# A two-layer transformer step on one core: low weight parts from a copy of the high parts in PSUM, and a seventh bank

## The chip, the cores and the metric

The kernel runs on one core of one Trainium2 chip. The metric is the device time of one execution in microseconds (us). Three runs of the kernel before gave 3073.89, 3075.67 and 3076.87 us; the median is 3075.67. One execution was also recorded by the hardware profiler, which gives the span and the rows below.

## What is computed

The reference is one inference step of a network of two layers for 128 context tokens and 512 sample tokens (together 640 columns) with 1024 features. Each layer has a half-step SwiGLU, a token mixer, and another half-step SwiGLU, so there are four half-steps in all. The part that the change is about is this (the mixers, attention with a long convolution in the first layer and a gated DeltaNet in the second, stay as they are):

```
def half_ffn(x, g, mod, j, w13, w2):
    gt, up = split(ada_norm(x, g, mod, j) @ w13, 2)      # 1024 -> 2 x 2816
    return x + 0.5 * gate * ((silu(gt) * up) @ w2)       # 2816 -> 1024
```

`ada_norm` is an RMS norm followed by a scale and a shift that come from a conditioning vector, one for the context tokens and one for the sample tokens. All of it is in float32.

## The kernel before

**Number format.** TensorE multiplies in a rounded format (float32r). To keep float32 accuracy each operand is split into a high part, which is the value rounded, and a low part, which is the value less the high part. A product is then three matmuls: high times high, high times low, low times high. The weights are split on the chip, unit by unit.

**The weight stream.** `w_ahead` (L430 to L457) converts weight units in the order in which the products use them, up to five slots ahead of TensorE, in a ring of six slots of 1024 columns (`wh`). A unit of the up projection is 128 x 512 (four tiles of 128 x 128). For it ScalarE writes the high part (L452) and VectorE subtracts it from the source and so writes the low part (L453). Both of the subtraction's operands lie in SBUF. For each pair of tiles GpSimd first makes four sums and differences of the weights (L447), from which four of the seven units are taken. A number called priority moves these two instructions 30 places ahead in the scheduler's order; the copies of L783 are moved by 150. The order of the instructions on each engine is fixed when the program is built, and each engine works through its own in order.

**Up stages.** `ffn_s` (L741 to L830) is one half-step. The 22 pairs of a gate tile and an up tile (128 features each) are done in chunks of 7, 7 and 8, the up stages. A pair is not four products of halves in eight parts but seven, of Strassen's kind: q = 0 to 6, each 12 matmuls of 128 x 322 (four operand tiles, three matmuls each). The 322 columns are one half of the tokens, 320, and two columns that carry the shift of the modulation through the product, one for context and one for sample tokens, which serve as the biases. The products run in the order 0, 3, 4, 1, 5, 2, 6, and in the first pair of a half-step in the order 0, 3, 1, 2, 4, 5, 6.

The results lie in PSUM banks: a (q = 0 and 1), c (q = 3 and 2), d (q = 4, and q = 6 again), e (q = 5). These are banks 4, 5, 6, 7, but in the second pair of a half-step 2, 3, 0, 1:

```
a, c, d, e = [self.ps[:, b, :] for b in ((2, 3, 0, 1) if ci == 0 and m == 1 else range(4, 8))]
dst = (a, a, c, c, d, e, d)[q]
```

What reads them, in the order of a pair: ScalarE copies the partial results of q = 0 and q = 3 to SBUF (L783). VectorE adds d to the first copy (L789) and does the two bias columns by themselves (L791). After q = 1 it multiplies a by the norm's factor (L798) and copies the bias (L800). After q = 5 it adds e (L793, bias L794), and GpSimd adds the second copy and multiplies by the factor (L795, L796). After q = 2 VectorE adds c (L802) and multiplies by the factor (L803), both into SBUF, and ScalarE applies SiLU in two pieces, to the 128 context columns (L804) and the 512 sample columns (L805). After q = 6 VectorE adds d (L807, bias L808) and GpSimd multiplies by the factor (L809). `finish` (L755 to L759) then multiplies the two branches (L756, L757), ScalarE rounds the result (L758) and VectorE makes its low part (L759); it runs in the next pair, at q = 3.

**Factors of the norm.** In half-steps 2 to 4 the norm's factors are made late: `make_rstd` (L697 to L713) runs after q = 4 of the first pair, with two matmul groups in banks 0 and 1, a square root on ScalarE (L708), two reciprocals (L709) and two products (L711) on VectorE. In the first half-step the factors are 1, and 48 pieces of the modulation (`ada_small`, L569 to L592) are computed beside the products, with banks 0 and 1 as their ring: small matmuls (L582), a copy by ScalarE (L584), a transpose by TensorE (L587).

**The stages that follow.** After each chunk come eight output tiles of the down projection, each in two banks (0 and 1, or 2 and 3; `wide`, L400 to L403; `gemm`, L473 to L486), added to the residual by three VectorE instructions (`x_add`, L734 to L738, recorded as L737). The second half-step's three up stages are at 1056 to 1163, 1212 to 1304 and 1352 to 1458 us of the span.

## Time and profile before

| | |
|---|---|
| median of three runs | 3075.67 us (3073.89 to 3076.87) |
| span of the profiled execution, which is its own time | 3072.3 us, 3.4 below that median |
| mean granted TensorE clock | 0.978 of full speed |
| instructions | 54018 |
| DMA | 300.80 MB, 98 GB/s on average |

PE is TensorE with its matmuls, PEld its weight loads, DVE is VectorE, ACT ScalarE, POOL GpSimd and SP the engine that issues the transfers. A group of instructions is named by its line, engine, operation and tiles, and has its count, busy time and mean duration; behind the last bar stands the idle time of the engine just before these instructions and what ended it. The releasers are inferred from semaphore events. The end of a pipelined matmul is modelled, so a group of matmuls can be drawn a little longer than the time until the next one starts. TensorE's granted clock is given in parts of its full speed.

### The profile page before, as it was taken

Reading aid. Unit: us, or ns where it says so; the run is one execution under the profiler, and the core shown is the slowest. Engines: PE = TensorE matmul, PEld = TensorE weight load, DVE = VectorE, ACT = ScalarE, POOL = GpSimd, SP = SyncE. Lnnn points to the kernel's source line nnn. Section 1 sums busy time; section 2 is a strip of 40 time slices with the busy share of each in tenths; the row PEclk is TensorE's granted clock in tenths of the full one; section 3 lists DMA queues with packets and bytes.
Section 4 is the critical chain, followed back from the end, with each engine's and each line's share of the span. In section 5 each row is a group of like instructions: output and inputs, shape, how many; then the busy total and the mean of one; then the engine's idle time right before and its main releaser. Section 6 shows DMA issues by size and latency. Waiting matters only on the chain. (4 is left out here: it accounts for less than half of the span.)

```text
span 3072.3 us, 54018 instructions
## 1 busy us (share of the span) xinstructions
PE 2903.3 (94%) x20612; PEld 2683.4 (87%) x20612; DVE 2263.2 (74%) x5235; ACT 1303.0 (42%) x2678; POOL 1158.2 (38%) x955
## 2 busy tenths in 40 slices
PE   5999999999989899999999999999998999999999
PEld 3999999977766899999899999978878888899999
DVE  6858586687865785858785858679898967858584
ACT  4424243466522342424342424445555544424241
POOL 3525253101222563535563535332222224626361
PEclk7999999999989999999999999999999999999999
DMA  5434353334375122222122222322211112222222
GB/s 202 141 107 150 105 158 121 122 105 125 100 274 206 63 72 84 85 74 89 50 74 85 84 75 84 131 91 70 72 59 34 34 37 94 68 77 74 84 70 83
DMA packets 109439, 300.80 MB, mean 98 GB/s; under 512 B 11803, under 2 KB 31963, under 8 KB 104444
## 3 DMA queue, kind: packets, MB, share of 16 engines
q1 hardware_dynamic: 109180, 297.35, 29.1%
q8 instruction: 162, 2.65, 0.4%
q14 instruction: 97, 0.79, 0.1%
HBM read 277.38 MB, written 19.93 MB: 97 GB/s over the span
## 5 line engine op out<-in xcount | busy, mean ns | idle before, releaser
L453 DVE TENSOR_TENSOR wh<-base,wh 128x512 fp32r<-128x512 f32 (+2 forms) x746 | 745.7, 1002 | 122.0 <-PE psum L482 62.6
L452 ACT ACTIVATE wh<-base 128x512 fp32r<-128x512 f32 (+2 forms) x779 | 533.7, 706 | 669.1 <-PE psum L482 400.8
L447 POOL TENSOR_TENSOR base<-base 128x512 f32<-128x512 f32 x352 | 518.1, 1476 | 683.9 <-DMA base<-w 364.1
L482 PE MATMUL psum<-G,wh 128*128 128x320 f32 x4992 | 742.5, 310 | 8.5 <-DVE base L737 8.0
L482 PEld LDWEIGHTS psum<-G,wh 128*128 128x128 f32 x4992 | 737.0, 188 | 13.4 <-issue 7.5
L778 PE MATMUL psum<-H,wh 128*128 128x322 f32 x4224 | 700.7, 317 | 22.6 <-ACT H L659 11.8
L778 PEld LDWEIGHTS psum<-H,wh 128*128 128x128 f32 x4224 | 648.0, 192 | 41.6 <-ACT H L659 13.8
L778 PE MATMUL psum<-HX,wh 128*128 128x322 f32 x3168 | 527.5, 316 | 27.5 <-DVE base L808 21.7
L778 PEld LDWEIGHTS psum<-HX,wh 128*128 128x128 f32 x3168 | 482.0, 191 | 44.0 <-issue 31.8
L482 PE MATMUL psum<-H,wh 128*128 128x322 f32 (+1 forms) x2448 | 476.7, 330 | 3.6 <-DVE base L722 2.1
L482 PEld LDWEIGHTS psum<-H,wh 128*128 128x128 f32 x2448 | 375.3, 193 | 25.8 <-issue 17.7
L737 DVE SCALAR_TENSOR_TENSOR base<-psum,base 128x128 f32<-128x128 f32 x336 | 127.1, 433 | 211.6 <-PE psum L482 211.5
L453 POOL TENSOR_TENSOR wh<-base,wh 128x1024 fp32r<-128x1024 f32 x33 | 82.2, 2491 | 239.5 <-ACT wh L452 234.8
L795 POOL TENSOR_TENSOR base<-base 128x320 f32<-128x320 f32 x88 | 113.1, 1285 | 143.4 <-DVE base L794 133.6
L805 ACT ACTIVATE base<-base 128x512 f32<-128x512 f32 x88 | 63.6, 723 | 204.0 <-DVE base L803 204.0
L758 ACT ACTIVATE G<-base 128x640 fp32r<-128x640 f32 x88 | 65.1, 740 | 167.0 <-DVE base L757 156.8
L756 DVE SCALAR_TENSOR_TENSOR base<-base 128x128 f32<-128x128 f32 x88 | 32.9, 374 | 120.0 <-POOL base L809 120.0
L694 POOL TENSOR_TENSOR base<-base 128x640 f32<-128x640 f32 x30 | 77.7, 2589 | 110.9 <-ACT base L692 94.7
L796 POOL TENSOR_TENSOR base<-base 128x320 f32<-128x320 f32 x88 | 87.8, 998 | 6.9
L809 POOL TENSOR_TENSOR base<-base 128x320 f32<-128x320 f32 x88 | 76.2, 866 | 28.9 <-DVE base L808 28.9
L803 DVE TENSOR_TENSOR base<-base 128x320 f32<-128x320 f32 x88 | 85.1, 967 | 0.4
L759 DVE TENSOR_TENSOR G<-base,G 128x640 fp32r<-128x640 f32 x88 | 71.8, 816 | 15.0 <-ACT G L758 14.9
(702 smaller groups left out, 3764.6 us busy)
## 6 DMA issues: line engine op xcount, KB each, us to landing
base<-w SPq DMA_DIRECT2D x208, 512.0 KB, 3.2
base<-ada_w SPq DMA_DIRECT2D x128, 256.0 KB, 3.7
base<-w SPq DMA_DIRECT2D x64, 448.0 KB, 3.3
base<-dn_in SPq DMA_DIRECT2D x33, 512.0 KB, 3.3
base<-ada_w SPq DMA_DIRECT2D x14, 1024.0 KB, 5.0
G<-ada_w SPq DMA_DIRECT2D x48, 256.0 KB, 3.5
HX<-ada_w SPq DMA_DIRECT2D x10, 1024.0 KB, 4.9
base<-mx_in SPq DMA_DIRECT2D x18, 512.0 KB, 3.3
```

What stands on the lines that cost most here:

```text
L447: nc.gpsimd.tensor_tensor(out=out, in0=x, in1=y, op=op)
L452: nc.scalar.activation(out=hi, in_=src, func=AF.Copy)
L453: (self.lo_eng if q is None else nc.vector).tensor_tensor(out=lo, in0=src, in1=hif, op=ALU.subtract)
L482: nc.tensor.matmul(ps[:, h, :n], lhsT=w[:, k, :], rhs=m[k][:, HALF * h:HALF * h + n], start=start and k == 0 and w is hi and m is mh, stop ...
L694: nc.gpsimd.tensor_tensor(out=self.acc.f, in0=self.acc.f, in1=sq, op=ALU.add)
L737: nc.vector.scalar_tensor_tensor(out=xt[:, xo:xo + n], in0=ps[:, h, o:o + n], scalar=gate[:, t, c:c + 1], in1=xt[:, xo:xo + n], op0=ALU.mu ...
L759: TT(out=gl[m], in0=tu, in1=gf[m], op=ALU.subtract)
L778: nc.tensor.matmul(dst[:, :HB], lhsT=w[:, i, :], rhs=v[:, i, :], start=not more and i == 0 and n == 0, stop=i == 3 and n == 2, skip_group_ ...
L795: nc.gpsimd.tensor_tensor(out=p5, in0=u2[:, 0, :HALF], in1=p5, op=ALU.add)
L796: nc.gpsimd.tensor_tensor(out=u2[:, 1, :HALF], in0=p5, in1=fac[:, 1], op=ALU.mult)
L803: TT(out=g2[:, 1, :HALF], in0=g2[:, 1, :HALF], in1=fac[:, 1], op=ALU.mult)
L809: nc.gpsimd.tensor_tensor(out=u2[:, 0, :HALF], in0=u2[:, 0, :HALF], in1=fac[:, 0], op=ALU.mult)
```

## The change

For up units (q is not None), while a flag `hi_ps` is set, ScalarE writes a second copy of the high part into PSUM, in bank 0 and bank 1 by turns, and VectorE subtracts this copy from the source. The flag is set in the up stages, but not in the first pair of half-steps 2 to 4, and it is cleared in the down projections. So the second pair of those half-steps can no longer use banks 0 and 1; it takes 2, 3, 6, 7, and its seventh product shares bank 6. All other pairs have bank 3 for the seventh product. The ring of the 48 modulation pieces moves to the four quarters of bank 2.

The bias columns are no longer handled by themselves: the buffers become 322 columns wide for each half, the factors have 1.0 in the two extra columns, and the evictions work on all 322. The four small instructions L791, L794, L800 and L808 are gone; the SiLU has three pieces (128, 192 and 320 columns). The sum with c is made in place in c's bank, and the product with the factor reads it from there. The two banks of an output tile are used as one run of columns, the last 320 of the first bank and the first 320 of the second, and `x_add` has two instructions. Comments and docstrings are left out in the new version.

```diff
             nc.scalar.activation(out=hi, in_=src, func=AF.Copy)
+            if q is not None and self.hi_ps:
+                cp = self.ps[:, self.w_conv % 2, :]
+                nc.scalar.activation(out=cp, in_=hif, func=AF.Copy)
+                hif = cp
             (self.lo_eng if q is None else nc.vector).tensor_tensor(out=lo, in0=src, in1=hif, op=ALU.subtract)
...
     def wide(self):
-        return self.ps[:, b:b + 2, :]
+        return self.ps[:, b:b + 2, :].rearrange("p b n -> p (b n)")[:, 512 - HALF:]
...
     def x_add(self, ps, t, gate, xt):
-        for (h, o, n, xo, c) in ((0, 0, NP, 0, 0), (0, NP, HALF - NP, NP, 1), (1, 0, HALF, HALF, 1)):
-            nc.vector.scalar_tensor_tensor(out=xt[:, xo:xo + n], in0=ps[:, h, o:o + n], scalar=gate[:, t, c:c + 1],
-                                           in1=xt[:, xo:xo + n], op0=ALU.mult, op1=ALU.add)
+        for c, v in enumerate((slice(0, NP), slice(NP, NT))):
+            nc.vector.scalar_tensor_tensor(out=xt[:, v], in0=ps[:, v], scalar=gate[:, t, c:c + 1], in1=xt[:, v], op0=ALU.mult, op1=ALU.add)
...
-        def finish(m, tg, tu, bu):
-            nc.vector.scalar_tensor_tensor(out=tu[:, :NP], in0=tu[:, :NP], scalar=bu[:, 0:1], in1=tg[:, :NP], op0=ALU.add, op1=ALU.mult)
-            nc.vector.scalar_tensor_tensor(out=tu[:, NP:], in0=tu[:, NP:], scalar=bu[:, 1:2], in1=tg[:, NP:], op0=ALU.add, op1=ALU.mult)
-            nc.scalar.activation(out=gh[m], in_=tu, func=AF.Copy)
-            TT(out=gl[m], in0=tu, in1=gf[m], op=ALU.subtract)
+        self.mm_i = 0
+
+        def finish(m, tg, tu):
+            for k, v in enumerate((slice(0, NP), slice(NP, NX))):
+                nc.vector.scalar_tensor_tensor(out=tg[:, v], in0=tu[:, v], scalar=tu[:, HALF + k:HALF + k + 1], in1=tg[:, v],
+                                               op0=ALU.add, op1=ALU.mult)
+            v = halves(tg)[:, :, :HALF]
+            nc.scalar.activation(out=halves(gh[m]), in_=v, func=AF.Copy)
+            TT(out=halves(gl[m]), in0=v, in1=halves(gf[m]), op=ALU.subtract)
...
-                a, c, d, e = [self.ps[:, b, :] for b in ((2, 3, 0, 1) if ci == 0 and m == 1 else range(4, 8))]
+                a, c, d, e, d2 = [self.ps[:, b, :] for b in ((2, 3, 6, 7, 6) if ti == 1 and not ready else (4, 5, 6, 7, 3))]
+                self.hi_ps = ready is not None or ti > 0
...
-                    dst = (a, a, c, c, d, e, d)[q]
+                    dst = (a, a, c, c, d, e, d2)[q]
...
-                        TT(out=g2[:, 1, :HALF], in0=d[:, :HALF], in1=p1[:, :HALF], op=ALU.add)
-                        bu = self.bias2()
-                        TT(out=bu, in0=d[:, HALF:HB], in1=p1[:, HALF:], op=ALU.add)
+                        TT(out=g2[:, 1], in0=d[:, :HB], in1=p1, op=ALU.add)
                     elif q == 5:
-                        TT(out=u2[:, 0, :HALF], in0=e[:, :HALF], in1=g2[:, 1, :HALF], op=ALU.add)
-                        TT(out=bu, in0=e[:, HALF:HB], in1=bu, op=ALU.add)
+                        TT(out=u2[:, 0], in0=e[:, :HB], in1=g2[:, 1], op=ALU.add)
                         nc.gpsimd.tensor_tensor(out=p5, in0=u2[:, 0, :HALF], in1=p5, op=ALU.add)
...
                     if q == 1 and not first or q == 5 and first:
-                        TT(out=g2[:, 0, :HALF], in0=a[:, :HALF], in1=fac[:, 0], op=ALU.mult)
-                        bg = self.bias2()
-                        nc.vector.tensor_copy(out=bg, in_=a[:, HALF:HB])
+                        TT(out=g2[:, 0], in0=a[:, :HB], in1=fac[:, 0], op=ALU.mult)
                     if q == 2 and not first or q == 5 and first:
-                        TT(out=g2[:, 1, :HALF], in0=c[:, :HALF], in1=g2[:, 1, :HALF], op=ALU.add)
-                        TT(out=g2[:, 1, :HALF], in0=g2[:, 1, :HALF], in1=fac[:, 1], op=ALU.mult)
-                        nc.scalar.activation(out=tg[:, :NP], in_=tg[:, :NP], func=AF.Silu, bias=bg[:, 0:1])
-                        nc.scalar.activation(out=tg[:, NP:], in_=tg[:, NP:], func=AF.Silu, bias=bg[:, 1:2])
+                        TT(out=c[:, :HALF], in0=c[:, :HALF], in1=g2[:, 1, :HALF], op=ALU.add)
+                        TT(out=g2[:, 1, :HALF], in0=c[:, :HALF], in1=fac[:, 1, :HALF], op=ALU.mult)
+                        for v, k in ((slice(0, NP), 0), (slice(NP, HALF), 1), (slice(HB, NX), 1)):
+                            nc.scalar.activation(out=tg[:, v], in_=tg[:, v], func=AF.Silu, bias=tg[:, HALF + k:HALF + k + 1])
                     if q == 6:
-                        TT(out=u2[:, 0, :HALF], in0=d[:, :HALF], in1=u2[:, 0, :HALF], op=ALU.add)
-                        TT(out=bu, in0=d[:, HALF:HB], in1=bu, op=ALU.add)
-                        nc.gpsimd.tensor_tensor(out=u2[:, 0, :HALF], in0=u2[:, 0, :HALF], in1=fac[:, 0], op=ALU.mult)
-                        tail = (m, tg, tu, bu)
+                        TT(out=u2[:, 0], in0=dst[:, :HB], in1=u2[:, 0], op=ALU.add)
+                        nc.gpsimd.tensor_tensor(out=u2[:, 0, :HALF], in0=u2[:, 0, :HALF], in1=fac[:, 0, :HALF], op=ALU.mult)
+                        tail = (m, tg, tu)
...
-                    s.ada_small([(0, j) for j in range(2, 8)], s.ring(0, 1), s.ada_bufs(arena, True)), ready)
+                    s.ada_small([(0, j) for j in range(2, 8)], s.ring(*[(2, 128 * i, 128) for i in range(4)]), s.ada_bufs(arena, True)), ready)
```

## Rows read from the trace of the kernel before

**Rows 1.** The page's totals: engine, busy us, share of the span, instructions.
```profile
PE 2903.3 (94%) x20612; PEld 2683.4 (87%) x20612; DVE 2263.2 (74%) x5235; ACT 1303.0 (42%) x2678; POOL 1158.2 (38%) x955
```

**Rows 2.** Busy time by stretch: stretch, its us, engines, granted clock, DMA share, GB/s.
```profile
1212.00:1304.00 92.00, 89.78 (x594) 88.18 (x593) 78.56 (x137) 41.76 (x79) 52.63 (x42) 1.00 0.25 78
...
2690.40:2693.80 3.40, 3.40 (x15) 3.40 (x14) 1.61 (x4) 0.00 (x0) 2.33 (x3) 0.51 0.00 0
```

**Rows 3.** Timeline of PE, half-step 2, chunk 2: start, us, group, count, idle before.
```profile
1224.46 3.75 PE L778 MATMUL psum<-H,wh 128*128 128x322 f32 x24
...
1237.00 3.75 PE L778 MATMUL psum<-H,wh 128*128 128x322 f32 x24
...
1253.59 2.02 PE L778 MATMUL psum<-HX,wh 128*128 128x322 f32 x12 [0.29 <-DVE base L808]
...
1267.63 2.02 PE L778 MATMUL psum<-HX,wh 128*128 128x322 f32 x12 [0.82 <-DVE base L808]
```

**Rows 4.** Waits of PE, whole run: us in total, times, longest us.
```profile
PE psum L778 <- DVE base L808: 21.7, 31, 2.3
...
PE psum L778 <- DVE base L791: 5.5, 6, 1.7
...
PE psum L587 <- ACT base L584: 2.5, 5, 0.7
PE psum L778 <- DVE base L802: 2.3, 10, 0.3
```

**Rows 5.** Groups of DVE, 1212 to 1303 us: count, busy us, mean ns, idle before.
```profile
L453 DVE TENSOR_TENSOR wh<-base,wh 128x512 fp32r<-128x512 f32 x45 | 45.2, 1007 | 3.8 <-PE psum L482 3.5 <-ACT wh L452 0.2
...
L803 DVE TENSOR_TENSOR base<-base 128x320 f32<-128x320 f32 x6 | 6.7, 1122 | 0.0
...
L793 DVE TENSOR_TENSOR base<-psum,base 128x320 f32<-128x320 f32 x7 | 3.3, 477 | 0.0
...
L756 DVE SCALAR_TENSOR_TENSOR base<-base 128x128 f32<-128x128 f32 x6 | 2.1, 352 | 10.8 <-POOL base L809 10.8
...
L791 DVE TENSOR_TENSOR base<-psum,base 128x2 f32<-128x2 f32 x7 | 1.0, 146 | 0.0
```

**Rows 6.** Two lines of DVE, whole run: count, shortest, median and longest ns.
```profile
L803 DVE TENSOR_TENSOR base<-base x88: 478/1102/1582, 79.3 to 3010.9; 128x320 f32<-128x320 f32 x88
...
L453 DVE TENSOR_TENSOR wh<-base,wh x746: 672/693/2586, 37.1 to 3048.0; 128x512 fp32r<-128x512 f32 x155, 128x896 fp32r<-128x896 f32 x16, 128x1024 fp32r<-128x1024 f32 x16
```

**Rows 7.** Groups of ACT, 1212 to 1303 us.
```profile
L452 ACT ACTIVATE wh<-base 128x512 fp32r<-128x512 f32 x43 | 25.4, 622 | 9.1 <-PE psum L778 8.2 <-issue 0.9
...
L805 ACT ACTIVATE base<-base 128x512 f32<-128x512 f32 x6 | 4.3, 723 | 19.0 <-DVE base L803 19.0
...
L783 ACT ACTIVATE base<-psum 128x322 f32<-128x322 f32 x7 | 2.9, 418 | 0.0
L804 ACT ACTIVATE base<-base 128x128 f32<-128x128 f32 x7 | 2.8, 404 | 10.7 <-DVE base L800 10.6
```

**Rows 8.** Timeline of PE, first chunk of half-step 4: the longest stop.
```profile
2689.88 3.10 PE L778 MATMUL psum<-HX,wh 128*128 128x322 f32 x12 [2.28 <-DVE base L808]
```

**Rows 9.** Timeline, first and second pair of half-step 2: start, us, group.
```profile
1078.93 4.17 DVE L709 RECIPROCAL base<-base 128x320 f32<-128x320 f32 x2 [0.31 <-ACT base L708]
...
1082.06 3.75 PE L778 MATMUL psum<-H,wh 128*128 128x322 f32 x24
...
1085.77 1.33 POOL L795 TENSOR_TENSOR base<-base 128x320 f32<-128x320 f32 x1
...
1087.37 0.48 DVE L807 TENSOR_TENSOR base<-psum,base 128x320 f32<-128x320 f32 x1
```

**Rows 10.** Groups of DVE, whole run, L737: count, busy us, mean ns.
```profile
L737 DVE SCALAR_TENSOR_TENSOR base<-psum,base 128x320 f32<-128x320 f32 x112 | 60.7, 542 | 0.0
L737 DVE SCALAR_TENSOR_TENSOR base<-psum,base 128x192 f32<-128x192 f32 x112 | 45.8, 409 | 0.0
L737 DVE SCALAR_TENSOR_TENSOR base<-psum,base 128x128 f32<-128x128 f32 x112 | 39.1, 349 | 211.6 <-PE psum L482 211.5
```

More of the change, by code (lines that the diff above doesn't have):

```diff
@@ L341, in __init__ @@
         self.modA = [arena.alloc(48) for _ in range(2)]
-        self.rstd, self.rms = [arena.alloc(NT) for _ in range(2)]
+        self.rstd, self.rms = [arena.alloc(2 * HB) for _ in range(2)]
+        nc.gpsimd.memset(self.rms.f[:, HALF:HB], 1.0)
         self.norm = self.rstd
@@ L357, in __init__ @@
         self.mm_i = 0
-        self.by_half = False
+        self.by_half = self.hi_ps = False
         self.lo_eng = nc.vector
@@ L361, in __init__ @@
         self.rg = self.ring(4, 5, 6, 7)
-        self.x_sc = nc.dram_tensor("x_scratch", (2, 128, (KT + 1) * NT), F32).ap()
+        self.x_sc = nc.dram_tensor("x_scratch", (2, 128, KT * NT + 2 * HB), F32).ap()
         self.k_sc = nc.dram_tensor("k_scratch", (2, 2, 128, 12 * 256), F32).ap()
@@ L481, in gemm @@
                         n = HALF + extra * h
-                        nc.tensor.matmul(ps[:, h, :n], lhsT=w[:, k, :], rhs=m[k][:, HALF * h:HALF * h + n],
+                        nc.tensor.matmul(ps[:, HALF * h:HALF * h + n], lhsT=w[:, k, :], rhs=m[k][:, HALF * h:HALF * h + n],
                                          start=start and k == 0 and w is hi and m is mh, stop=stop and k == nk - 1 and w is lo)
@@ L637, in new_s @@
         if self.sums is None:
-            self.sums, self.fac = [self.A.arenas[0].alloc(n, True) for n in (2048, NT)]
+            self.sums, self.fac = [self.A.arenas[0].alloc(n, True) for n in (2048, 2 * HB)]
+            self.nc.gpsimd.memset(self.fac.f[:, HALF:HB], 1.0)
     def make_s(self, t, l, j, xt, tmp, sq, n=HB):
@@ L649, in make_s @@
             nc.vector.scalar_tensor_tensor(out=e[:, h, o:o + m], in0=xt[:, xo:xo + m], scalar=a[:, t, c:c + 1],
-                                           in1=self.rstd.f[:, xo:xo + m], op0=ALU.mult, op1=ALU.mult)
+                                           in1=self.rstd.f[:, xo + 2 * h:xo + 2 * h + m], op0=ALU.mult, op1=ALU.mult)
         for h in range(2) if n > HALF else ():
@@ L706, in make_rstd @@
         for h in range(2):
-            c = slice(HALF * h, HALF * h + HALF)
+            c = slice(HB * h, HB * h + HALF)
             nc.scalar.activation(out=rms.f[:, c], in_=p[:, h, :HALF], func=AF.Sqrt, scale=1.0 / D, bias=self.c("eps"))
@@ L721, in scaled @@
             c = slice(HALF * h, HALF * h + HALF)
-            nc.vector.tensor_tensor(out=out[:, c], in0=ps[:, h, :HALF], in1=self.norm.f[:, c], op=ALU.mult)
+            nc.vector.tensor_tensor(out=out[:, c], in0=ps[:, c], in1=self.norm.f[:, HB * h:HB * h + HALF], op=ALU.mult)
         if not self.by_half:
-            nc.vector.tensor_tensor(out=out.rearrange("p (h n) -> p h n", h=2), in0=ps[:, :, :HALF],
-                                    in1=self.norm.f.rearrange("p (h n) -> p h n", h=2), op=ALU.mult)
+            nc.vector.tensor_tensor(out=out.rearrange("p (h n) -> p h n", h=2), in0=ps[:, :NT].rearrange("p (h n) -> p h n", h=2),
+                                    in1=self.norm.f.rearrange("p (h n) -> p h n", h=2)[:, :, :HALF], op=ALU.mult)
         b = self.bias2()
-        nc.vector.tensor_copy(out=b, in_=ps[:, 1, HALF:HALF + 2])
+        nc.vector.tensor_copy(out=b, in_=ps[:, NT:NX])
         return b
@@ L749, in ffn_s @@
         part = [A.alloc(n, True) for n in (HB, HALF)]
-        tmp = [[A.alloc(NT, True) for _ in range(2)] for _ in range(2)]
+        tmp = [[A.alloc(2 * HB, True) for _ in range(2)] for _ in range(2)]
         xv = self.x.f.rearrange("p (t n) -> p t n", n=NT)
@@ L764, in ffn_s @@
                 p1, p5, tg, tu = [b.f for b in part + tmp[ti % 2]]
+                g2, u2 = halves(tg), halves(tu)
+                first = ci == 0 and m == 0
+                a, c, d, e, d2 = [self.ps[:, b, :] for b in ((2, 3, 6, 7, 6) if ti == 1 and not ready else (4, 5, 6, 7, 3))]
+                self.hi_ps = ready is not None or ti > 0
                 ti += 1
-                g2, u2 = halves(tg), halves(tu)
-                a, c, d, e = [self.ps[:, b, :] for b in ((2, 3, 0, 1) if ci == 0 and m == 1 else range(4, 8))]
-                first = ci == 0 and m == 0
                 for q in FIRST if first else REST:
@@ L795, in ffn_s @@
                         nc.gpsimd.tensor_tensor(out=p5, in0=u2[:, 0, :HALF], in1=p5, op=ALU.add)
-                        nc.gpsimd.tensor_tensor(out=u2[:, 1, :HALF], in0=p5, in1=fac[:, 1], op=ALU.mult)
+                        nc.gpsimd.tensor_tensor(out=u2[:, 1, :HALF], in0=p5, in1=fac[:, 1, :HALF], op=ALU.mult)
                     if q == 1 and not first or q == 5 and first:
-                        TT(out=g2[:, 0, :HALF], in0=a[:, :HALF], in1=fac[:, 0], op=ALU.mult)
-                        bg = self.bias2()
@@ L813, in ffn_s @@
                         tail = None
+            self.hi_ps = False
             last = ci == len(FCH) - 1
@@ L1478, in norm_load @@
     def norm_load(self, l):
-        self.rms, self.acc = [self.A.arenas[0].alloc(NT, True) for _ in range(2)]
+        self.rms, self.acc = [self.A.arenas[0].alloc(n, True) for n in (2 * HB, NT)]
         self.nc.sync.dma_start(out=self.rms.f, in_=self.x_sc[l, :, KT * NT:])
```

## The prediction

> **What bounds the kernel now.** I read the engines' totals first: TensorE (PE) is busy 94% of the span and VectorE (DVE) 74% [rows 1]. The table by stage shows that the change lies in a stretch where the two are close: in the second up stage of the second half-step PE works 89.8 of 92.0 us and DVE 78.6, while ScalarE (ACT) works 41.8 [rows 2]. Next I read PE's own timeline there. Early in the chunk a pair of tiles (seven products, 84 matmuls) takes 1237.00 − 1224.46 = 12.54 us, 149 ns for a matmul, with no gap; a little later one takes 1267.63 − 1253.59 = 14.04, and the bracket names L808 [rows 3]. So PE sets the time until DVE falls behind; then the seventh product, which writes the fifth's bank again, waits until DVE has read that bank. The waits of PE give the whole price: L808 ends 21.7 us of idle time in 31 stops, L791 (the same bank, read one product earlier) 5.5 in 6, L802 2.3 in 10 [rows 4]. That is 29.5 us in 47 stops. It is too little by what the view cannot see: 24 matmuls are drawn 3.75 us long although the next follow 2/7 × 12.54 = 3.58 after their start [rows 3], so a stop begins 0.17 earlier than drawn. 47 × 0.17 = 8.0 makes it 37.5 us.
>
> **What the change does to DVE.** Per pair DVE has 7 subtractions L453 at a mean 1007 ns, L803 at 1122, four two-column instructions at 146, six reads or sums near 480, and the finish [rows 5]; the stage's 78.56 us over seven pairs are 11.22 each [rows 2]. Of 12.54 that is too much, since there are waits as well: 10.8 us in six pairs for POOL's L809 before L756 [rows 5], 1.8 a pair. The durations have two levels. L453 and L803 read SBUF twice and spread upwards from 672 and from 478, L803 to a median of 1102 [rows 6], while L793, of the same 320 columns but with one operand in PSUM, has a mean of 477, just L803's minimum [rows 5, 6]. I take it that two SBUF operands make DVE lose time to POOL, which sums weights meanwhile, and that one operand in PSUM frees it. No row shows a 512-column subtraction from PSUM. From above it is bounded by today's 1007, from below by 672; I take 680, as L793 sits at the lower level in all its forms. DVE per pair: 11.22 − 7 × 0.33 − (1.12 − 0.48) for L803, which now reads PSUM, − 0.3 for the four small ones (0.58, of which two eviction columns more and overlaps give some back) = 8.0 us, between 7.9 and 10.3.
>
> The Trainium skill ("Perfetto Trace Analysis", section "Optimizing Scalar/DVE Operations") puts VectorE's access overhead at about 60 ns on SBUF and 125 on PSUM, so by it each moved subtraction would be some 65 ns dearer: 8.0 + 7 × 0.065 = 8.4 us a pair, an estimate. L793 and L803's minimum, 477 and 478, show no such difference [rows 5, 6]. Either way DVE stays under 12.54, and nothing below rests on this paragraph.
>
> **What it does to ACT.** Per pair ACT works 41.76 / 7 = 5.97 us. Added are 7 copies of 512 columns into PSUM. No row shows ACT writing PSUM; the copy into SBUF, L452, is 622 [rows 7], and L783, which reads PSUM, does 322 columns in 418, so 512 would be 418 + 190 × 0.83 = 576 at the slope of a column. I take 620: 4.3 us. The SiLU in three pieces instead of two adds 404 + 128 and 192 to 320 columns' worth against 404 + 723 [rows 7], 0.3. The sum is 10.6 of 12.54 (10.3 with 576). It hides beside PE as long as ACT's waits in its own order for L800 and L803 (10.7 and 19.0 us in seven pairs, 4.2 a pair [rows 7]) become places where a copy fits, or shorten with DVE's chain. Without that cover the sum is 14.8, and ACT is the bound (third rival).
>
> **What is removed from PE's path.** The seventh product has a bank of its own, so the L808 and L791 stops go. Only in the second pair of half-steps 2 to 4 does it still share (bank 6): 3 of 66 pairs, 1.7 us. What L802 stopped goes with DVE's lead. −36 us. One long stop, 2.28 us before 2689.88, also cost clock [rows 8]: behind it the granted clock was 0.51 for 3.4 us, near 1.2 of the two levels 1.2 and 2.4 GHz, with 15 matmuls where 149 ns each would give 23 [rows 2]. 8 × 0.149 = 1.2 us comes back: −1.2.
>
> **What is new on it.** In half-steps 2 to 4 the second pair takes banks 2, 3, 6, 7, and its second product (q=3) writes bank 3, which the first pair's seventh has just filled. So it waits for L807 of the first pair, which today frees nobody early. In half-step 2 PE could start q=3 at 1082.06 + 1.79 = 1083.85; L807 starts at 1087.37 [rows 9], behind two reciprocals (4.17 us from 1078.93), the scaling, L793, L798, L802 and L803, and behind POOL's L795, which reads what L807 overwrites and ends at 1085.77 + 1.33 = 1087.10 [rows 9]. L803 shrinks, L795 does not: L807 ends near 1087.4. 3.5 us, three times: +10.5. If the order puts L807 first it is 0 (first rival); with the wait behind a slower L453 it is 4.5 each, so 0 to 13.5. Each such stop is longer than that of rows 8, so the clock should fall too; 1.2 us three times with a discount of a third, since one of them may meet a clock still high: +2.5 (0 to 3.6).
>
> In the first half-step 48 pieces of the modulation run beside the products, and PE waits there for ACT's L584 2.5 us in five of them [rows 4]. Copies of 0.62 can now stand before it: between 0 and 48 × 0.62 = 30; since only five pieces wait today, 5 × 0.62 = +3. That these pieces share one bank costs nothing I can see, as the same ACT read frees each quarter.
>
> The residual update's three instructions (349 + 409 + 542 ns) become two, the 320-column one at 542 growing to 512 by 192 × 1.0 = 735 [rows 10]: 1300 − 1084 = 0.22 less, on the path at the end of each of four half-steps, elsewhere under PE: −0.8. Wider buffers, factors of 1.0 and memsets are set once and cost nothing beside this. The weights' DMAs and POOL's sums (L447) are issued as before; SP's and POOL's queues keep their order.
>
> **Sum.** −36 − 1.2 + 10.5 + 2.5 + 3 − 0.8 = −22.0. The profiled execution's span is 3072.3, 3.4 under the median of the runs, 3075.67; I subtract from the median: 3053.7, so **3054**. The bounds of the terms (new stops 0 to 13.5, clock 0 to 3.6, pieces 0 to 10 if only a third of the bound comes) give 3043 to 3063 for this case alone, as not all go one way.
>
> **Rivals.** (1) *No new stop.* The order of DVE moves L807 before the reciprocals' followers, and POOL's L795 earlier. For it: the order is the scheduler's, and L793 has no need of the reciprocals. Against it: L795 waits for POOL's L447. −36 − 1.2 + 3 − 0.8 = −35: 3041. Chance 0.13. (2) *C's bank takes over.* The third sum is now made in place in C's bank, which is free only after L803, 0.48 us later than after L802. L802 stops PE today in 10 pairs [rows 4]; if 31 pairs, as many as stop at L808, are late by 0.48, 14.9 us come back: 3069. Against it: DVE at 8.0 of 12.54 is not late. Chance 0.18. (3) *ScalarE becomes the bound (slower).* With 10.6 us of work and 4.2 of waits kept in order, the copy that L453 now waits for arrives late, and PE waits for weights. It decides from the period of a pair: the stage read here has a mean of 92 / 7 = 13.14 us [rows 2], and I take that for the 45 pairs of chunks two and three in the last three half-steps; a period over it loses. At 13.8, that is 14.8 with 1.0 of the 4.2 us of waits filled, 45 × 0.66 = 30 us are lost there; the first chunks keep their 21 of 66 pairs' share of the gain, 11.5; with the new stops (13), the pieces (3) and the rest (−2) it comes to 3108. For it: the waits are real today. Against it: they are idle time with nothing to do, since L452 waits for PE to free a slot (8.2 of its 9.1 us [rows 7]). Chance 0.14. (4) *The subtraction gets no faster*, since POOL and DVE contend in PSUM cases too or the lower level is not reached: the bank and small instructions alone act, DVE at 10.3 plus waits of 1.8 just keeps up; two thirds of 36 goes, −24 − 1.2 + 13 + 3 − 0.8 = −10: 3066. Chance 0.05.
>
> **Chances.** Forecast 0.50, rivals 0.13, 0.18, 0.14, 0.05. A difference under 0.2%, 6.2 us, can't be told from none here; the limits are 3069.5 and 3081.8. Faster: 0.50 + 0.13 + 0.10 (half of rival 2) + 0.04 = 0.77. Same: the rest of rival 2 and 4, and 0.02 of rival 3: 0.11. Slower: 0.12. The range runs from 3036, 5 under rival 1, to 3074, 5 over rival 2; it leaves out rival 3 and some 0.04 under it.
>
> **What would show it.** Right: L453 in one narrow peak near 680; DVE near 8 us a pair; pairs of 12.54 to the chunk's end; no stop at the seventh product's bank; three stops near 3.5 us before q=3 of the second pair, released by the line that was L807, with a granted clock near 0.5 behind them; ACT near 10.6 a pair. Wrong: PE waits named L452, L453 or the new copy (rival 3), L803 (rival 2), L584 by more than 10 us (the pieces), or L453 still at 900 and more (rival 4).

## The result and the profile after

The kernel after takes 3025.86 us (median of four runs, 3023.93 to 3027.96), the kernel before 3075.48 beside it; the ratio is 0.9835, with a 95% interval of 0.9821 to 0.9849. That is 50 us less. The forecast had the sign right and the size wrong: 3054, with a range that ended at 3036.

The page's totals of the kernel after, which answer to [rows 1]:

```profile
span 3023.0 us, 54115 instructions
...
PE 2887.1 (96%) x20612; PEld 2686.1 (89%) x20612; DVE 2058.8 (68%) x4771; ACT 1642.4 (54%) x3325; POOL 1094.3 (36%) x958
```

TensorE has the same 20612 matmuls and weight loads. VectorE is busy 204 us less, ScalarE 339 us more. Now the busy time of the second and third up stage of half-step 2, and of a stretch in the second mixer (columns as in [rows 2]):

```profile
1203.00:1291.20 88.20, 88.20 (x593) 88.20 (x593) 62.14 (x107) 68.91 (x129) 47.13 (x42) 1.00 0.25 81
1340.60:1441.10 100.50, 100.50 (x675) 100.50 (x675) 71.66 (x128) 80.70 (x150) 56.03 (x49) 1.00 0.26 87
2094.70:2115.20 20.50, 20.50 (x176) 18.13 (x176) 9.99 (x26) 10.31 (x39) 2.94 (x4) 0.50 0.00 1
```

In both up stages PE is busy all the time. A pair leaves VectorE 62.14 / 7 = 8.9 us of work (it was 11.2) and ScalarE 68.91 / 7 = 9.8 (it was 6.0). The third row is a stretch in which PE worked at half its clock (granted 0.50); it is not in the profile of before, and there is more on it below. The timeline of PE in the second up stage, which answers to [rows 3], shows the pitch of a pair:

```profile
1228.31 3.75 PE L787 MATMUL psum<-H,wh 128*128 128x322 f32 x24
1231.90 1.95 PE L787 MATMUL psum<-HX,wh 128*128 128x322 f32 x12
...
1240.86 3.75 PE L787 MATMUL psum<-H,wh 128*128 128x322 f32 x24
1244.44 1.94 PE L787 MATMUL psum<-HX,wh 128*128 128x322 f32 x12
```

1240.86 − 1228.31 = 12.55 us, and it stays so to the end of the chunk. The waits of PE on products of the up projection, which answer to [rows 4]:

```profile
PE psum L787 <- ACT base L792: 8.6, 6, 2.2
...
PE psum L787 <- ACT H L665: 5.6, 5, 2.5
...
PE psum L787 <- DVE base L807: 0.2, 1, 0.2
```

L792 is the copy that was L783, and L665 was L659; both of these waits lie in the first pair of a half-step, where the operands are still being made. Of 29.5 us of waits for evictions by VectorE 0.2 are left. The groups of the second up stage, for [rows 5] and [rows 7] (L458 is the subtraction that was L453, L456 the copy into PSUM, L453 the high part that was L452, L807 was L803, L767 was L759):

```profile
L458 DVE TENSOR_TENSOR wh<-base,psum 128x512 fp32r<-128x512 f32 x45 | 30.8, 686 | 14.7 <-ACT psum L456 10.6 <-PE psum L487 3.1
...
L453 ACT ACTIVATE wh<-base 128x512 fp32r<-128x512 f32 x43 | 26.9, 625 | 7.4 <-PE psum L787 6.8 <-POOL base L448 0.5
L456 ACT ACTIVATE psum<-wh 128x512 f32<-128x512 f32 x43 | 25.9, 602 | 1.1
...
L767 DVE TENSOR_TENSOR G<-base,G 128x640 fp32r<-128x640 f32 x6 | 6.0, 995 | 1.3 <-ACT G L766 1.3
...
L807 DVE TENSOR_TENSOR base<-psum,base 128x320 f32<-128x320 f32 x6 | 3.0, 493 | 0.2
```

The subtraction from PSUM takes 686 ns where the old one took 1007, and L807 493 where L803 took 1122. The spread over the whole run answers to [rows 6] (shortest, median and longest):

```profile
L458 DVE TENSOR_TENSOR wh<-base,psum x559: 672/686/692, 35.9 to 2953.7; 128x512 fp32r<-128x512 f32 x187
...
L458 DVE TENSOR_TENSOR wh<-base,wh x187: 676/1083/2594, 158.2 to 2998.6; 128x1024 fp32r<-128x1024 f32 x66, 128x896 fp32r<-128x896 f32 x64, 128x512 fp32r<-128x512 f32 x57
```

All 559 subtractions from PSUM lie within 20 ns of each other. The second row mixes three widths. By width, the 57 of 512 columns that are still done from SBUF, 46 of them with GpSimd idle, take 676 to 693 ns; those of 896 and 1024 columns are as spread as before (1078 to 1892 and 1162 to 2594, before 1077 to 1915 and 1162 to 2586).

**Where the time went.** The span is cut at the first and last matmul of each up stage. All runs of this study are in the table, so that one can see which stages an edit touched (us; the parts are those of the profiled execution, the median is over the timed runs, and each session had the kernel before beside it at 3073 to 3076):

| run | median | up stages, half-step 1 | first chunks, half-steps 2–4 | chunks 2 and 3, half-steps 2–4 | rest of the span |
|---|---|---|---|---|---|
| before | 3075.48 | 325.6 | 324.1 | 594.3 | 1828.3 |
| after | 3025.86 | 322.0 | 301.4 | 565.4 | 1834.2 |
| no_copy | 3087.21 | 329.5 | 322.1 | 595.6 | 1823.9 |
| shared_bank | 3019.18 | 320.9 | 303.4 | 565.6 | 1830.0 |
| neither | 3080.59 | 328.9 | 322.3 | 594.3 | 1831.6 |
| held_order | 3037.09 | 320.0 | 315.7 | 565.5 | 1821.5 |
| no_copy_no_sums | 3003.90 | 319.0 | 290.3 | 565.5 | 1825.9 |
| two_copies | 3039.76 | 319.5 | 311.1 | 573.3 | 1832.5 |
| banked_wide | 3015.87 | 320.1 | 303.8 | 565.5 | 1821.4 |
| first_no_copy | 3033.77 | 330.2 | 299.8 | 565.5 | 1841.5 |
| after_again | 3022.24 | 323.4 | 302.8 | 565.5 | 1836.3 |
| banked_shared | 3022.88 | 320.2 | 302.1 | 565.5 | 1830.7 |
| no_sums | 3004.42 | 319.8 | 291.5 | 565.5 | 1826.8 |
| first_banks | 3021.35 | 320.1 | 303.1 | 565.5 | 1826.2 |

The up stages of half-steps 2 to 4 gave 22.7 + 28.9 = 51.6 us, the first half-step 3.6; the rest became 5.9 longer. 565.4 us for 45 pairs are 12.56 a pair: there is nothing left to gain there beside the matmuls themselves. The rest of the span varies by 20 us from program to program without any edit in it, so the medians are not good to more than some 10 us where programs differ; the stages' own times are steadier, and the experiments are read from them. Chunks 2 and 3 repeat within 0.2 us wherever PE has no stop; the first chunks took 301.4 and 302.8 in two executions of the same program (after and after_again), the first half-step's stages 322.0 and 323.4.

### The profile page after: what moved, and what is told of

Its sections match the earlier page's. It is cut to its first block, busy times and chain, and to the rows that moved or that the text cites. A ratio compares the mean times of both kernels' runs of the same rounds, so it can differ in the third digit from the quotient of the medians.

```text
span 3023.0 us, 54115 instructions
## 1 busy us (share of the span) xinstructions
PE 2887.1 (96%) x20612; PEld 2686.1 (89%) x20612; DVE 2058.8 (68%) x4771; ACT 1642.4 (54%) x3325; POOL 1094.3 (36%) x958
## 5 line engine op out<-in xcount | busy, mean ns | idle before, releaser
L453 ACT ACTIVATE wh<-base 128x512 fp32r<-128x512 f32 (+2 forms) x779 | 546.0, 706 | 600.5 <-PE psum L487 390.3
L448 POOL TENSOR_TENSOR base<-base 128x512 f32<-128x512 f32 x352 | 494.3, 1409 | 660.8 <-DVE wh L458 365.1
L787 PEld LDWEIGHTS psum<-H,wh 128*128 128x128 f32 x4224 | 648.4, 192 | 28.7 <-ACT base L792 10.6
L458 DVE TENSOR_TENSOR wh<-base,psum 128x512 fp32r<-128x512 f32 x559 | 381.4, 684 | 152.7 <-ACT psum L456 119.1
L456 ACT ACTIVATE psum<-wh 128x512 f32<-128x512 f32 x559 | 334.6, 600 | 45.9 <-DVE base L743 26.1
L458 DVE TENSOR_TENSOR wh<-base,wh 128x896 fp32r<-128x896 f32 (+2 forms) x187 | 202.1, 1085 | 91.2 <-PE psum L487 37.2
L743 DVE SCALAR_TENSOR_TENSOR base<-psum,base 128x128 f32<-128x128 f32 x224 | 113.0, 547 | 218.0 <-PE psum L487 218.0
L763 DVE SCALAR_TENSOR_TENSOR base<-base 128x128 f32<-128x128 f32 (+1 forms) x176 | 96.1, 552 | 123.1 <-POOL base L812 122.9
L458 POOL TENSOR_TENSOR wh<-base,wh 128x1024 fp32r<-128x1024 f32 x33 | 82.7, 2507 | 240.8 <-ACT wh L453 236.1
L801 POOL TENSOR_TENSOR base<-base 128x320 f32<-128x320 f32 x88 | 82.0, 932 | 161.4 <-DVE base L800 99.6
L809 ACT ACTIVATE base<-base 128x128 f32<-128x128 f32 (+2 forms) x264 | 114.8, 469 | 35.2 <-DVE base L804 17.4
L700 POOL TENSOR_TENSOR base<-base 128x640 f32<-128x640 f32 x30 | 76.3, 2544 | 112.1 <-ACT base L698 109.2
L767 DVE TENSOR_TENSOR G<-base,G 128x640 fp32r<-128x640 f32 x88 | 85.3, 969 | 21.5 <-ACT G L766 21.2
L812 POOL TENSOR_TENSOR base<-base 128x320 f32<-128x320 f32 x88 | 77.8, 884 | 44.0 <-DVE base L811 39.0
```

The costliest lines, as they stand in the source:

```text
L448: nc.gpsimd.tensor_tensor(out=out, in0=x, in1=y, op=op)
L453: nc.scalar.activation(out=hi, in_=src, func=AF.Copy)
L456: nc.scalar.activation(out=cp, in_=hif, func=AF.Copy)
L458: (self.lo_eng if q is None else nc.vector).tensor_tensor(out=lo, in0=src, in1=hif, op=ALU.subtract)
L743: nc.vector.scalar_tensor_tensor(out=xt[:, v], in0=ps[:, v], scalar=gate[:, t, c:c + 1], in1=xt[:, v], op0=ALU.mult, op1=ALU.add)
L763: nc.vector.scalar_tensor_tensor(out=tg[:, v], in0=tu[:, v], scalar=tu[:, HALF + k:HALF + k + 1], in1=tg[:, v], op0=ALU.add, op1=ALU.mult)
```

## The experiments

Two theories stood at the start. L: VectorE's load in the up stages decides, and it is the subtraction's duration that changed it. B: the bank which two products shared decides. The second is what the prediction charged the 36 us to.

**no_copy**

```diff
-                self.hi_ps = ready is not None or ti > 0
+                self.hi_ps = False
```

> The new kernel with the flag never set, so that every subtraction reads SBUF twice again; the own bank, the wide evictions and the in-place sum stay. Theory L (VectorE's load decides): the 512-column subtraction goes back to about 1000 ns, VectorE from 8.8 to about 11 us a pair, and with 1.6 us of waits for GpSimd it is late again: 15 to 30 us of the 50 are lost, 3040 to 3055. Theory B (the shared bank decides): the bank of the seventh product no longer waits, so a late VectorE reaches TensorE only through other banks, and under 8 us are lost, at most 3034.

Measured: 3087.21 us, ratio 1.0034 to the kernel before (1.0011 to 1.0057). All is lost, more than theory L asked, although the own bank stayed. The waits of PE show how:

```profile
PE psum L787 <- DVE base L807: 30.3, 36, 1.9
...
PE psum L787 <- ACT base L792: 9.0, 7, 2.2
...
PE psum L787 <- DVE base L811: 5.0, 3, 1.8
```

The stops that stood at the shared bank (L808 and L791, 27.2 us) now stand at c's bank, which L807 frees: 30.3. It is the very mechanism of the second rival. A late VectorE is met at whichever bank comes next; the own bank only chose another one. L811, the eviction of the seventh product, stops PE only behind the second pair of half-steps 2 to 4, where that product still shares bank 6.

**shared_bank**

```diff
-                a, c, d, e, d2 = [self.ps[:, b, :] for b in ((2, 3, 6, 7, 6) if ti == 1 and not ready else (4, 5, 6, 7, 3))]
+                a, c, d, e, d2 = [self.ps[:, b, :] for b in ((2, 3, 6, 7, 6) if ti == 1 and not ready else (4, 5, 6, 7, 6))]
```

> The new kernel with the seventh product in the fifth's bank again (bank 6), copies as they are. Theory L: a VectorE with 8.8 us of work in 12.5 reads the bank in time, no more than 6 us are lost: 3024 to 3032. Theory B: the order of the instructions on VectorE alone makes the fifth product of the next pair late, and 20 to 35 us come back: 3045 to 3060.

Measured: 3019.18 us, 0.9815 (0.9790 to 0.9840), and 303.4 + 565.6 us in the up stages against 301.4 + 565.4. With the copies the own bank is worth 2.2 us by these stages, 0.7 by those of after_again, and the median of the whole run is not longer without it. Theory B is out.

**neither**

```diff
-                a, c, d, e, d2 = [self.ps[:, b, :] for b in ((2, 3, 6, 7, 6) if ti == 1 and not ready else (4, 5, 6, 7, 3))]
-                self.hi_ps = ready is not None or ti > 0
+                a, c, d, e, d2 = [self.ps[:, b, :] for b in ((2, 3, 6, 7, 6) if ti == 1 and not ready else (4, 5, 6, 7, 6))]
+                self.hi_ps = False
```

> The new kernel without the copies and with the shared bank: what the wide evictions, the sum in place and the two-instruction residual update do by themselves. Theory L and theory B alike: near the kernel before, 3060 to 3075; if the small instructions were what made VectorE late (0.6 us a pair), 3035 to 3050.

Measured: 3080.59 us, 1.0017 (1.0003 to 1.0031), 916.6 us in those up stages (before 918.4); the median lies 6 us over the range expected. The wide evictions, the sum in place and the two-instruction update do nothing by themselves, though they take four instructions a pair from VectorE. The reverse, the copies without these edits, was not run.

**held_order.** The prediction's stop before the second product of the second pair didn't appear in the kernel after. There TensorE's own order had changed:

```profile
1078.11 1.96 PE L787 MATMUL psum<-H,wh 128*128 128x322 f32 x12
1079.90 1.94 PE L787 MATMUL psum<-HX,wh 128*128 128x322 f32 x12
1081.68 1.94 PE L787 MATMUL psum<-H,wh 128*128 128x322 f32 x12
1083.46 1.04 PE L787 MATMUL psum<-HX,wh 128*128 128x322 f32 x6
1084.35 1.95 PE L787 MATMUL psum<-H,wh 128*128 128x322 f32 x12
```

Products q = 0 and 3 read H, q = 4 reads HX. The first line is q = 0; behind it comes not q = 3 but q = 4, then q = 1 and half of q = 5, and only then, at 1084.35, q = 3. The detour goes with bank 3. In shared_bank, neither and banked_shared the first pair's seventh product is not in that bank, and there 36 matmuls that read H stand in a row at this place, as in shared_bank:

```profile
1077.32 5.53 PE L787 MATMUL psum<-H,wh 128*128 128x322 f32 x36
```

So what was free was put before the product whose bank was taken. This run holds the written order:

```diff
-                            nc.tensor.matmul(dst[:, :HB], lhsT=w[:, i, :], rhs=v[:, i, :], start=not more and i == 0 and n == 0,
+                            mm = nc.tensor.matmul(dst[:, :HB], lhsT=w[:, i, :], rhs=v[:, i, :], start=not more and i == 0 and n == 0,
...
+                    if q == 3 and ti == 2 and not ready:
+                        held = self.tc.issue_after(mm.ins)
+                        held.__enter__()
+                    elif q == 6 and ti == 2 and not ready:
+                        held.__exit__(None, None, None)
```

> The new kernel with TensorE held to the written order 0, 3, 4, 1, 5, 2, 6 in the second pair of half-steps 2 to 4, where the scheduler had put the second product behind the fourth. If the step of the prediction was right but for the order, three stops of 1 to 3.7 us appear before the second product of that pair, released by the eviction of the first pair's seventh (L811), with the clock at half behind some: 3 to 13 us are lost, 3029 to 3039. If that eviction is early in any case, nothing is lost: 3024 to 3028.

Measured: 3037.09 us (3024.42 to 3040.28), and the first chunks 315.7 against 301.4: 14.3 us, a little over what was expected. The timeline of PE, and the stretch behind it:

```profile
1076.16 1.95 PE L787 MATMUL psum<-H,wh 128*128 128x322 f32 x12
1081.37 2.72 PE L787 MATMUL psum<-H,wh 128*128 128x322 f32 x12 [3.25 <-DVE base L816]
```
```profile
1082.40:1085.80 3.40, 3.40 (x15) 3.40 (x14) 1.36 (x3) 1.12 (x2) 1.20 (x2) 0.50 0.44 154
```

L816 is this kernel's line for the eviction that was L807. There are three such stops, 9.8 us in all (10.5 were predicted, and drawn waits are short by 0.17 each), and the granted clock was 0.50 for 3.4 us behind each of the three. The place, the releaser and the price of the predicted stop were right; that the written order would be kept was not.

**no_copy_no_sums.** Why is a subtraction from SBUF slow? Theory P says that GpSimd's work makes it so, theory S that two reads of SBUF are slow in any case. In the trace of before the 616 subtractions of 512 columns can be sorted by whether GpSimd worked during them, and so can the new ones (worked out from their start and end times; an overlap under 3% counts as idle, one of 98% or more as throughout):

| | GpSimd idle | busy for a part | busy throughout |
|---|---|---|---|
| before, both operands in SBUF | 312, mean 682 ns, longest 695 | 228, mean 1207 | 76, mean 1280 |
| after, one operand in PSUM | 292, mean 685, longest 691 | 100, mean 683 | 167, mean 685 |

That is a correlation in the same program. The run takes most of GpSimd's work away, and with it the copies; it leaves out the sums of all pairs but the first of each half-step, so that it no longer computes the reference:

```diff
-        self.sums = self.fac = None
+        self.sums = self.fac = self.sums_made = None
...
-                if q == 0:
+                if q == 0 and self.sums is not self.sums_made:
+                    self.sums_made = self.sums
...
-                self.hi_ps = ready is not None or ti > 0
+                self.hi_ps = False
```

> As no_copy, and GpSimd's sums of the weights are made for the first pair of each half-step alone; the later pairs take these old sums, so the products of the later pairs are not the reference's. Theory P (a subtraction with two SBUF operands is slow only while GpSimd works): the mean of the 512-column subtraction falls from about 900 to 700 to 800 ns, the twelve up stages come near those of the new kernel, and the time is 3025 to 3045. Theory S (reading SBUF twice is slow for VectorE in any case, or contends with TensorE or ScalarE): the mean stays above 850 and the time at 3075 to 3090.

Measured: 3003.90 us, 0.9770 (0.9749 to 0.9791), and 565.5 us for chunks two and three. The group of the subtractions in a stretch of 91 us:

```profile
L459 DVE TENSOR_TENSOR wh<-base,wh 128x512 fp32r<-128x512 f32 x36 | 27.0, 750 | 0.3
```

750 ns with both operands in SBUF: GpSimd still has its three operations on the evictions of each pair. Theory P holds, theory S does not. The time is 21 us below what theory P had asked. Against the kernel after the first half-step's stages are 3.0 us shorter and the first chunks 11.1. All of the latter lies in the three first pairs, where the flag is off in every run: 63.7 us against 74.8, with 10.2 us at half clock against 23.9. By half the difference some 7 of the 11.1 are the clock (an estimate). So the sums cost time there too, which the change does not reach; by which wait was not traced.

**no_sums** is the same edit on the kernel after, copies included.

> The new kernel, copies included, with GpSimd's sums made for the first pair of each half-step alone; the later pairs' products are not the reference's. If the copies act only by taking VectorE out of GpSimd's way (theory P), they are worth next to nothing here: 2995 to 3008, within 8 us of no_copy_no_sums (3003.9). If a subtraction from PSUM is quicker in itself, 2980 or less.

Measured: 3004.42 us, 0.5 us from the run without copies. Where GpSimd's sums are out of the way the copies are worth nothing: what they do is to take VectorE out of GpSimd's way.

**two_copies**

```diff
                 nc.scalar.activation(out=cp, in_=hif, func=AF.Copy)
+                nc.scalar.activation(out=cp, in_=hif, func=AF.Copy)
```

> The new kernel with each copy into PSUM made twice. ScalarE goes from 9.8 to 14.1 us of work a pair. If it becomes the bound (the third rival's mechanism), a pair takes 14.1 to 15.5 us instead of 12.55 and the twelve up stages together lose 80 to 250 us: 3105 to 3275. If the copies run far enough ahead, or the second one falls into idle time, 3024 to 3040.

Measured: 3039.76 us, 0.9893 (0.9875 to 0.9911); the up stages of half-steps 2 to 4 lose 17.6 us, far less than 80. ScalarE is at its limit, and yet it hardly holds up the rest, as the stretch 1210 to 1290 us and the waits of PE show (L459 is the subtraction here):

```profile
1210.00:1290.00 80.00, 79.41 (x532) 79.14 (x531) 58.74 (x97) 79.10 (x160) 44.09 (x40) 1.00 0.23 74
```
```profile
PE psum L788 <- DVE wh L459: 10.6, 18, 0.6
```

ScalarE is busy 79.1 of 80 us: its waits in its own order, 4.2 us a pair before, are all filled. In the kernel after it is busy 68.9 of 88.2, so it had room for most of a second copy. Even with that copy ScalarE works 86.0 us of the 88.8 of this stage, 12.3 a pair and not the 14.1 expected.

**first_no_copy**

```diff
-                self.hi_ps = ready is not None or ti > 0
+                self.hi_ps = ready is None and ti > 0
```

> The new kernel without copies in the first half-step. By the prediction's step for the modulation's pieces 3 us are gained there: its three up stages together 319, the time 3021 to 3025. By the trace of the new kernel, whose first half-step became shorter, 3 to 8 us are lost: 325 to 330 together, 3028 to 3034.

Measured: 3033.77 us; the first half-step's up stages take 330.2 us instead of 322.0. The step of the prediction had the wrong sign. PE's wait for the modulation's copy (L584, now L589) is longer without the copies:

```profile
PE psum L592 <- ACT base L589: 5.3, 6, 1.6
```

It is 0.4 us in one wait in the kernel after, and was 2.5 in five before [rows 4]. So the copies do not delay these pieces; that they stand behind a late VectorE was not shown by itself.

**banked_wide, banked_shared, after_again.** The mixers were longer after the change (a rest of 1834.2 us against 1828.3), and the layout of the output tiles is the edit that reaches them. banked_wide goes back to two separate banks and three instructions in the residual update; banked_shared undoes the seventh bank as well; after_again is the kernel after once more.

```diff
-        return self.ps[:, b:b + 2, :].rearrange("p b n -> p (b n)")[:, 512 - HALF:]
+        return self.ps[:, b:b + 2, :]
...
-        for c, v in enumerate((slice(0, NP), slice(NP, NT))):
+        for (h, o, n, xo, c) in ((0, 0, NP, 0, 0), (0, NP, HALF - NP, NP, 1), (1, 0, HALF, HALF, 1)):
...
```

> The new kernel with an output tile's halves at the start of two banks as before and three instructions in the residual update. By the prediction 0.8 us are lost on the path: 3025 to 3029. If the new layout is what made the two mixers 6.6 us longer than before, 3016 to 3021.

> The new kernel with the seventh product in the fifth's bank and the output tiles' halves at the start of two banks: both parts undone that cost nothing one by one. If the copies alone make the gain, 3012 to 3028 and the up stages of half-steps 2 to 4 near 868 together. If one part stands in for the other, 3030 or more.

> The new kernel once more, beside the three others. In its first profile the second mixer had a stretch of 20.5 us at half clock that the kernel before has not. If that stretch is an accident of one execution, it is gone or elsewhere and the time is 3016 to 3028; if it belongs to this program, it is there again, near 2095 us, and the time is 3024 to 3028.

Measured: 3015.87, 3022.88 and 3022.24 us, with ratios to before whose intervals overlap (0.9794 to 0.9830, 0.9805 to 0.9858, 0.9804 to 0.9859). banked_wide alone would have spoken for the layout; with the same layout and one more part undone the gain is gone again, so the layout is not shown to cost anything. What varies is mostly how long the clock is low. The rest of the span has 75.5 and 77.2 us at half clock where it is 1821 us long (held_order, banked_wide), 111.8 and 120.5 where it is 1836 and 1842 (after_again, first_no_copy). The profiled executions before and after have 93.6 and 104.2, and half of these 10.6 us would be 5.3 of the 5.9 by which the rest was longer. The 20.5 us at half clock near 2095 us are not in after_again, which has 27 us at half clock from 2447 to 2475 instead. So stretches of that length came and went between two executions of one program; at half of their length they cost 10 to 14 us each, an estimate.

**first_banks.** The waits for L792 that remain in the kernel after (8.6 us) come from q = 1 and 2 being summed onto q = 0 and 3 in the banks of a and c, once ScalarE has copied those. This run gives q = 1 and 2 of the first pair banks of their own, on the layout of banked_wide.

```diff
-                a, c, d, e, d2 = [self.ps[:, b, :] for b in ((2, 3, 6, 7, 6) if ti == 1 and not ready else (4, 5, 6, 7, 3))]
+                own = first and not ready
+                a, c, d, e, d2 = [self.ps[:, b, :] for b in ((4, 5, 6, 7, 6) if own else (4, 5, 6, 7, 3))]
+                a1, c1 = [self.ps[:, b, :] for b in (3, 2)] if own else (a, c)
...
-                    dst = (a, a, c, c, d, e, d2)[q]
-                    more = q in (1, 2)
+                    dst = (a, a1, c1, c, d, e, d2)[q]
+                    more = q in (1, 2) and not own
...
+                        if own:
+                            TT(out=a1[:, :HB], in0=a1[:, :HB], in1=p1, op=ALU.add)
+                            TT(out=c1[:, :HALF], in0=c1[:, :HALF], in1=p5, op=ALU.add)
+                            a, c = a1, c1
```

> The layout of banked_wide, and in the first pair of half-steps 2 to 4 the products q = 1 and 2 have banks of their own (3 and 2), so that they need not wait for ScalarE's copies of q = 0 and 3 (8.6 us in six stops in the new kernel); two more sums on VectorE, and the second pair uses the usual banks. If these stops are what is late there, the three first chunks lose 6 to 10 us: 3006 to 3014. If the operands come no earlier than the copies, the stops get another name and nothing is gained: 3014 to 3024.

Measured: 3021.35 us, first chunks 303.1 (banked_wide 303.8). Nothing is gained in all. The longest stops of the first pairs are for the operands, which L665 makes:

```profile
PE psum L790 <- ACT H L665: 9.4, 5, 3.0
...
PE psum L790 <- DVE base L814: 2.4, 9, 0.4
...
PE psum L790 <- DVE base L818: 1.8, 3, 0.6
```

In the kernel after the wait for L665 was 5.6 us. But banked_wide, whose layout this run shares, has 11.9 us of it already, and 0.8 for the copies, so there was little for the banks to take away, and the new name is not their doing. What the edit did is to move time: the three first pairs are 7.8 us shorter than in banked_wide (69.8 against 77.6, with 20.5 us at half clock against 27.3), while the second pairs are 2.5 longer (40.0 against 37.5) and the third 1.8 (39.4 against 37.6), with stops at evictions by VectorE (L814 and L818) which banked_wide has not. It has two more sums to do there; that these make it late was not tested by itself.

No run that computes the whole step is shown to be faster than the kernel after; the two runs near 3004 us leave sums out.

## Why the prediction was right and wrong

**Right: what bounds the kernel, and the durations.** PE set the time until VectorE fell behind. The subtraction was put at 680 ns and takes 686, the in-place sum's second half at 480 and takes 493. VectorE was put at 8.0 us a pair and has 8.9. Of the 0.9 some 0.2 is L767 (before L759, 814 ns), which now takes 995, and another 0.2 that the stage holds 45 of the cheaper subtractions and not 49; the rest was not traced. ScalarE was put at 10.6 and has 9.8, as the stage holds 43 copies and not 49 (0.5) of 602 ns and not 620 (0.1). The rule of the Trainium skill that was weighed there ("Perfetto Trace Analysis", "Optimizing Scalar/DVE Operations") would have made the subtraction some 65 ns dearer; with GpSimd idle it is 685 from PSUM and 682 from SBUF, so the row was the better guide.

**Wrong: the new stop, +10.5 and +2.5.** The step read "its second product (q=3) writes bank 3 … So it waits for L807 of the first pair". held_order shows the stop and its price, 14.3 us with the clock against the 13.0 forecast; in the kernel after it is nothing. But I took the order of TensorE's instructions from the source. It is the scheduler's too, as I had said of VectorE's in the first rival, and an order that changes with the banks is no fixed term of the sum. The first rival came true, but by PE going round the stop: in half-step 2 the eviction (now L811) starts 4.6 us after the second pair's first product, and before the change it was 5.3.

**Wrong in size: −36 for the stops.** The up stages of half-steps 2 to 4 gave 51.6, the forecast's stops and the clock together 37.2. Of the difference of 14.4 us 3.4 lie in the first pairs (78.2 us in three before, 74.8 after), which I had not entered, and some 11 in stops that the waits view doesn't show in full. The 3.4 are no sure gain of the change: these pairs had 30.7 us at half clock before and 23.9 after, and after_again, the same program, has 27.3 and takes 76.3. The third chunk of half-step 2 tells it. It took 105.55 us and takes 100.54, so 5.0 were lost. PE's waits there, before, and those of its weight loads:

```profile
PE psum L778 <- DVE base L808: 2.8, 4, 0.8
PE psum L778 <- DVE base L802: 0.3, 1, 0.3
```
```profile
PEld psum L778 <- issue: 4.9, 8, 1.1
```

Five stops of 3.1 us, with 0.17 each 4.0; the weight loads show eight stops and 4.9 us, which is the loss. Shorter stops have no row with a releaser (at 1405.40 and 1433.40 a matmul starts 253 and 200 ns over the pitch of 149, and the wait is drawn as 94 and 41), and behind each stop the next matmul is some 75 ns late as well (at 1394.30 and 1394.52, 449 and 74 ns over the pitch). The better estimate was the plainest one: the length of the stage less 84 × 0.149 us a pair.

**Wrong cause: "the seventh product has a bank of its own, so the L808 and L791 stops go".** They go because VectorE is no longer late; the bank without the copies gives nothing (no_copy), and the copies without the bank give nearly all (shared_bank). The fourth rival, a bank without a faster subtraction, was priced at 3066, while no_copy takes 3087. I had read the releaser's name as the cause. I had also put the L808 stops at the wrong product: the stop of 1253.59 in [rows 3] stands behind 24 matmuls that read H (q = 0 and 3), so it is q = 4 of the next pair, in the same bank d, that waits for the eviction of q = 6.

```profile
1249.55 3.75 PE L778 MATMUL psum<-H,wh 128*128 128x322 f32 x24
```

**Wrong sign: +3 for the modulation's pieces.** The first half-step became 3.6 us shorter, and without copies there it is 8.2 longer than with them.

**Not resolved: −0.8 for the residual update.** The runs can't tell it from nothing.

**The other rivals.** C's bank did take over, but only in no_copy, where VectorE was late. ScalarE as the bound did not appear: with every copy made twice it was busy 79.1 of 80 us, and even then the loss in those up stages was 17.6 us: its waits in order were places for copies, and not a sum to be added to its work.

Together: 3053.7 less 13.0 (the stop and its clock) less 14.4 (stops and first pairs) less 6.6 (the first half-step, 3.0 + 3.6) is 3019.7; the rest of the span took back 5.9, and the residual update's 0.8, and that gives 3026.4 against 3025.86. That it closes so well is in part luck, since the 5.9, and the 3.4 of the first pairs in the 14.4, are mostly the clock of these two executions.

## What to carry to other kernels

When several waits on one engine name different lines of the same late engine, price them as one lag: ask whether the late engine catches up, and don't credit a change that only gives one of the waiting places more room. Take what a bound engine loses from the length of the stage against its own pitch, since short stops are missing from the waits, and read the order of every engine's instructions as something that a scheduler may turn when a bank moves. Where one kind of instruction has two durations, sort it by what another engine did at the time before looking for a cheaper form.

## What the runs showed of the hardware

A VectorE subtraction with both operands in SBUF takes nearly twice as long in the mean while GpSimd works (682 against 1280 ns for 512 columns), and with one operand in PSUM it shows no difference (685 and 685). Not every work of GpSimd counts the same: of the subtractions that lay beside a single GpSimd instruction for over half of their time, 92 beside L447 (the weights' sums) took 1528 ns in the mean, six beside L694 (a sum of 640 columns) took 681. GpSimd gains as well: its 320-column sum (L795, now L801) took 1257 ns in the second up stage of half-step 2 and takes 879. TensorE's clock stayed at half for 20.5 us while PE was busy throughout; behind the same wait of 1.00 us before L1734 (now L1738), in the same work, it fell in the first execution of the kernel after and in neither the second nor that of the kernel before.
